# Feed-forward, MLP and output products: one 512-column product per high weight tile in place of two of 256

## The chip, the cores and the metric

The kernel runs on one core of a Trainium2 chip (trn2). The metric is the device time of one execution in microseconds. TensorE multiplies, a stationary operand (weight load) against a moving one whose columns stream through, and adds up in PSUM banks of 512 float32 columns; VectorE and ScalarE read those banks; GpSimd does small work; SyncE issues the weight transfers.

## The reference

Two transformer blocks, one after the other, on one sequence of 256 tokens and 1024 features, all in float32. The first has an attention with compressed, selected and windowed keys beside a gated linear recurrence, then a squared-ReLU MLP; the second has a feed-forward, two attentions (a two-dimensional neighbourhood and a window with a sink), and a second feed-forward. Cut to the products of the change:

```python
def first_block(x, ...):                      # D_MODEL 1024, SEQ 256, D_FF 4096
    ...
    x = x + merged @ w_out[l]
    hn = rms_norm(x, norm2_w[l])
    x = x + jnp.square(jax.nn.relu(hn @ mlp_w1[l])) @ mlp_w2[l]
    return rms_norm(x, final_norm_w)

def swiglu(x, w_gate, w_up, w_down):          # D_FF_2 2816
    return (jax.nn.silu(x @ w_gate) * (x @ w_up)) @ w_down

def second_block(h, ...):
    h = h + 0.5 * swiglu(rms_norm_2(h, ffn1_norm[l]), ffn1_w_gate[l], ffn1_w_up[l], ffn1_w_down[l])
    ...
    h = h + merged @ w_out[l]
    h = h + 0.5 * swiglu(rms_norm_2(h, ffn2_norm[l]), ffn2_w_gate[l], ffn2_w_up[l], ffn2_w_down[l])
    return rms_norm_2(h, final_norm)
```

## The kernel before

Activations lie feature-major: a tile of 128 features by T = 256 tokens. Each float32 operand is cut into a high part, rounded to the format that TensorE multiplies at full rate (float32r), and a low part, the rest. A product W x is then the sum of three: high W by high x, high W by low x, low W by high x. `mm3` (line 271 in the profile) issues these three, each with its own weight load and 256 columns, into one half of a bank: a bank holds a pair of output tiles, 2 x 256 columns. The names in the profile: `f` are the gate and up products of the two feed-forwards (`u2` and `u4` are their inputs, `h` high and `l` low), `fd` the first one's down product, `w` both products of the MLP (inputs `u1` and `hid`), `wo` the two output projections (inputs `m1`, `m2`), `ld` the last down product, which is the other way round: activations stationary, weights moving, 512 columns at first.

Weights stream from memory in pieces of 1024 columns (eight blocks of 128 x 128). For each piece ScalarE makes the high part `whi` (line 221) and VectorE the low part `wlo` (line 222); five of each are kept, and a piece is cut two ahead in program order. A scheduler sets the order on each engine; engines run their queue in order.

When a pair's sum is complete it is read: in the MLP one VectorE operation takes the ReLU and the norm factor `rb_A` (line 1061), ScalarE squares, and both cut the result into the parts of `hid`. In a feed-forward the gate side is multiplied by the norm factor (line 1161), goes through SiLU on ScalarE and is multiplied again (line 1163); the up side is multiplied by it (line 1168) and cut (`f1hi`, `f1lo`). `fm` does products whose sum is added to the residual `res` (line 1041 for `wo`). After `wo`, `w`'s second product and `fd` a norm follows: sums of squares `acc`, a product `ssq_acc` that adds them up over partitions, a small chain of VectorE and GpSimd, and a broadcast `bc_A` on TensorE. The products that need the norm start on features 0 to 5 of 8 before the last two are there.

PSUM has four pools: `g` three banks, `s` two, `t` two, `o` one. Feature-major products take `g`; the up side of a feed-forward takes `s`, which else holds attention scores; `o` holds attention outputs. Line 820, in the first attention, multiplies probabilities of 2 x 384 columns of which it takes the first 256 of each, so that its 512 moving columns are two runs.

Of the kernel before, what the change touches and what calls it, by code (L numbers as in the profile page):

```python
# [9 lines left out]
F32R = mybir.dt.float32r  # L10
# [4 lines left out]
P = 128  # L15
T = 256
# [55 lines left out]
# ------------------------------------------------------------------ constants  # L72
# [81 lines left out]
# Order of the first block's products and of the work between them; "at" takes items of the attention's list.  # L154
# [7 lines left out]
# -------------------------------------------------------------------- program  # L162
class Prog:
    def __init__(self, nc, tc, ctx_pools, d, dbg=None):
# [4 lines left out]
        self.groups = []  # L169

# [61 lines left out]
    def behind(self, ins, before):  # L232
        """keeps ins behind another instruction of its engine"""
# [5 lines left out]
    def table(self, group, **kw):  # L239
        """An activation whose function table is shared by a group: groups are issued in the order of the program."""  # L240
# [22 lines left out]
    def mm3(self, out, wh, wl, xh, xl, start, stop, wside=True):  # L263
        """out += W^T x with operands in two exact parts (W stationary, or x when wside is False)."""
        mm = self.nc.tensor.matmul
        if wside:
            seq = ((wh, xh), (wh, xl), (wl, xh))
        else:
            seq = ((xh, wh), (xh, wl), (xl, wh))
        for r, (a, b) in enumerate(seq):  # L270
# [1280 lines left out]
```

## Time and profile before

| | us |
|---|---|
| three runs, median (lowest to highest) | 994.73 (992.94 to 994.96) |
| profiled execution, span | 992.9 |
| TensorE busy | 982.1 (99%) |
| VectorE busy | 676.7 (68%) |
| ScalarE busy | 549.6 (55%) |
| GpSimd busy | 39.3 (4%) |

The span runs from the first to the last instruction of the profiled execution; the profile has no other time for that execution, and its span lies 1.9 us under the median of the runs. Products on TensorE are pipelined: one is listed at 0.28 us, but the next starts 0.12 us after it, so it is the distance of starts that tells what one costs. The granted clock is at its upper level nearly throughout (mean 0.994).

### The profile page before, as it was taken

The numbers are of one execution on the slowest core, as the hardware profiler recorded it, in microseconds if no ns is written. First come the engines' busy times: TensorE is split into PE (matmuls) and PEld (weight loads), VectorE is DVE, ScalarE is ACT, GpSimd is POOL, SyncE is SP. The second block draws the span as 40 slices with busy tenths as digits, with TensorE's granted clock in tenths as the row PEclk, the third lists the DMA queues.
The fourth block names the chain that finished last, engine by engine and source line by source line (L and its number), as shares of the span: only waits on it lengthen the run. The fifth ranks groups of instructions, "written<-read, shape, count | busy, mean of one in ns | idle before, by whom it ended". The sixth has DMA issues, their size and how long they took to land.

```text
span 992.9 us, 18648 instructions
## 1 busy us (share of the span) xinstructions
PE 982.1 (99%) x7830; PEld 959.4 (97%) x7830; DVE 676.7 (68%) x1051; ACT 549.6 (55%) x833; POOL 39.3 (4%) x71
## 2 busy tenths in 40 slices
PE   8999999999999999999999999999999999999997
PEld 7999999999999999999999999999899999999897
DVE  7898779668666545577666556778767766656453
ACT  6784798446655444455444444667664554444441
POOL 6100000000000000020000200000000000000000
PEclk9999999999999999999999999999999999999999
DMA  8585423635545544555455655442235555555541
GB/s 322 182 296 185 149 105 121 233 127 197 185 170 177 199 177 175 194 176 210 173 196 184 205 191 186 166 170 98 93 108 173 192 204 175 176 200 174 175 154 43
DMA packets 26564, 174.20 MB, mean 175 GB/s; under 512 B 3312, under 2 KB 3568, under 8 KB 7280
## 3 DMA queue, kind: packets, MB, share of 16 engines
q1 hardware_dynamic: 24912, 169.80, 48.2%
q0 software_dynamic: 1136, 2.63, 1.3%
q8 instruction: 61, 1.00, 0.4%
q10 hardware_dynamic: 432, 0.58, 0.2%
q14 instruction: 23, 0.19, 0.1%
HBM read 171.43 MB, written 1.05 MB: 174 GB/s over the span
## 4 chain that ended last, share of the span: by engine, by line
PE 96%; ACT 2%; DVE 1%; DMA 1%; issue 0%; POOL 0%; POOLq 0%; ACTq 0%
PE f L271 26%; PE w L271 19%; PE fd L271 6%; PE ld L271 6%; PE ga L271 5%; PE gb L271 5%; PE wo L271 5%; PE gr L271 3%; PE m1b L271 2%; PE xr L271 2%; PE va L271 1%; PE qb L271 1%; PE qa L271 1%; PE ka L271 1%; PE m1a L271 1%; PE m2b L271 1%
## 5 line engine op out<-in xcount | busy, mean ns | idle before, releaser
L221 ACT ACTIVATE whi<-raw 128x1024 fp32r<-128x1024 f32 (+3 forms) x322 | 336.3, 1048 | 365.2 <-PE f L271 96.2
L222 DVE TENSOR_TENSOR wlo<-raw,whi 128x1024 fp32r<-128x1024 f32 (+3 forms) x322 | 388.6, 1210 | 187.2 <-ACT whi L221 184.3
L271 PE MATMUL f<-u4l,whi 128*128 128x256 f32 x352 | 99.8, 283 | 0.0
L271 PE MATMUL f<-u2h,whi 128*128 128x256 f32 x352 | 99.8, 283 | 0.0
L271 PE MATMUL f<-u4h,wlo 128*128 128x256 f32 x352 | 99.6, 283 | 0.0
L271 PE MATMUL f<-u4h,whi 128*128 128x256 f32 x352 | 99.6, 283 | 0.0
L271 PE MATMUL f<-u2l,whi 128*128 128x256 f32 x352 | 99.6, 283 | 0.0
L271 PE MATMUL f<-u2h,wlo 128*128 128x256 f32 x352 | 99.6, 283 | 0.0
L271 PE MATMUL w<-u1h,wlo 128*128 128x256 f32 x256 | 72.6, 284 | 0.0
L271 PE MATMUL w<-hid_hi,whi 128*128 128x256 f32 x256 | 72.4, 283 | 0.0
L271 PE MATMUL w<-hid_lo,whi 128*128 128x256 f32 x256 | 72.4, 283 | 0.0
L271 PE MATMUL w<-hid_hi,wlo 128*128 128x256 f32 x256 | 72.4, 283 | 0.0
L271 PE MATMUL w<-u1h,whi 128*128 128x256 f32 x256 | 72.4, 283 | 0.0
L271 PE MATMUL w<-u1l,whi 128*128 128x256 f32 x256 | 72.4, 283 | 0.0
L271 PEld LDWEIGHTS f<-u4h,wlo 128*128 128x128 f32 x352 | 67.6, 192 | 0.0
L271 PEld LDWEIGHTS f<-u2l,whi 128*128 128x128 f32 x352 | 67.6, 192 | 0.0
L271 PEld LDWEIGHTS f<-u4h,whi 128*128 128x128 f32 x352 | 67.6, 192 | 0.0
L271 PEld LDWEIGHTS f<-u2h,whi 128*128 128x128 f32 x352 | 67.6, 192 | 0.0
L271 PEld LDWEIGHTS f<-u4l,whi 128*128 128x128 f32 x352 | 67.6, 192 | 0.0
L271 PEld LDWEIGHTS f<-u2h,wlo 128*128 128x128 f32 x352 | 67.6, 192 | 0.0
L271 PE MATMUL fd<-f1hi,whi 128*128 128x256 f32 x176 | 49.8, 283 | 0.0
L271 PE MATMUL fd<-f1lo,whi 128*128 128x256 f32 x176 | 49.8, 283 | 0.0
(598 smaller groups left out, 2746.1 us busy)
## 6 DMA issues: line engine op xcount, KB each, us to landing
raw<-in_ws_dram SPq DMA_DIRECT2D x150, 1024.0 KB, 4.9
raw<-in_ws_dram SPq DMA_DIRECT2D x3, 960.0 KB, 4.8
raw<-in_ws_dram SPq DMA_DIRECT2D x2, 992.0 KB, 5.2
nar<-in_rpb_dram POOLq DMA_DIRECT2D x16, 96.0 KB, 5.4
raw<-in_ws_dram SPq DMA_DIRECT2D x4, 256.0 KB, 7.2
raw<-in_ws_dram SPq DMA_DIRECT2D x2, 512.0 KB, 7.3
raw<-in_ws_dram SPq DMA_DIRECT2D x1, 932.0 KB, 4.8
res<-in_x_dram SPq DMA_DIRECT2D x2, 384.0 KB, 7.0
```

Source lines behind the costliest of these rows:

```text
L221: self.hi_ins.append(nc.scalar.activation(out=hi[:, :w], in_=src, func=AF.Copy))
L222: nc.vector.tensor_tensor(out=lo[:, :w], in0=src, in1=hi[:, :w].bitcast(F32), op=ALU.subtract)
L271: mm(out, a, b, start=start and r == 0, stop=stop and r == 2, skip_group_check=True)
```

## The change

A block's two products with the high weight become one: the two parts of an activation lie behind one another in one buffer (`Parts`: per four feature tiles one buffer, high parts in the first half, low parts in the second), and both stream past one weight load as 512 columns, two runs of 256 (`mm_wide`). High by high lands in the first half of a bank, high by low in the second; the product with the low weight adds 256 columns to the first half. So an output tile takes a whole bank and a pair two. `banks` takes them in rotation from `g`, `g`, `g`, `s`, `s`, `o`. Whoever reads a pair now sums the halves: `fold` lets ScalarE copy the second half to SBUF and VectorE add the first; `add_res` adds both halves to the residual one after the other. This is done for `wo`, `w`, `f` and `fd`; all other feature-major products keep three products per block (`mmx`). Comments are taken out, and the buffers of parts of other operands (`u0`, `xcp`, `rnn`, `ya`, `yb`, ...) are cut in the new way too.

```diff
+WIDE = ("g", "g", "g", "s", "s", "o")
+class Parts:
+    def buf(self, k):
+        while len(self.bufs) <= k // 4:
+            self.bufs.append(self.big(f"{self.name}_{len(self.bufs)}", F32R, (P, 2, 4, T)))
+        return self.bufs[k // 4]
+    def both(self, k):
+        return self.buf(k)[:, :, k % 4, :]
...
+    def mm_wide(self, bank, wh, wl, x, start, stop):
+        mm = self.nc.tensor.matmul
+        mm(bank.rearrange("p (a t) -> p a t", a=2), wh, x, start=start, stop=False, skip_group_check=True)
+        mm(bank[:, :T], wl, x[:, 0, :], start=False, stop=stop, skip_group_check=True)
+
+    def banks(self, name):
+        out = []
+        for nn in range(2):
+            tag = WIDE[self.n_wide % len(WIDE)]
+            self.n_wide += 1
+            out.append(self.ps(tag, f"{name}_{nn}"))
+        return out
+
+    def fold(self, out, bs):
+        for nn, b in enumerate(bs):
+            o = out[:, nn * T:(nn + 1) * T]
+            self.nc.scalar.activation(out=o, in_=b[:, T:], func=AF.Copy)
+            self.nc.vector.tensor_tensor(out=o, in0=b[:, :T], in1=o, op=ALU.add)
...
 (fm, fm_norm, ffn)
-                    st[p] = self.ps(pool, f"{tag}_{p}")
-                b = st[p]
+                    st[p] = self.banks(f"{tag}_{p}")
                 for k in range(k0, k1):
-                    xh, xl = x(k)
                     for nn in range(2):
                         wh, wl = self.wt((tag, k, 2 * p + nn))
-                        self.mm3(b[:, nn * T:(nn + 1) * T], wh, wl, xh, xl, k == 0 and nn == 0, k == nk - 1)
+                        self.mm_wide(st[p][nn], wh, wl, x(k), k == 0, k == nk - 1)
...
+    def add_res(p, bs, fac):
+        for nn, b in enumerate(bs):
+            r = S["res"][:, 2 * p + nn, :]
+            for a in range(2):
+                nc.vector.scalar_tensor_tensor(out=r, in0=b[:, a * T:(a + 1) * T], scalar=fac, in1=r, op0=ALU.mult, op1=ALU.add)
...
-    def ev_mlp(p, b):
+    def ev_mlp(p, bs):
...
-        nc.vector.scalar_tensor_tensor(out=v2(r), in0=v2(b), scalar=0.0, in1=two(S["rbA"]), op0=ALU.max, op1=ALU.mult)
+        G.fold(r, bs)
+        nc.vector.scalar_tensor_tensor(out=v2(r), in0=v2(r), scalar=0.0, in1=two(S["rbA"]), op0=ALU.max, op1=ALU.mult)
...
-        def ev(p, side, b):
+        def ev(p, side, bs):
...
-                nc.vector.tensor_tensor(out=v2(s), in0=v2(b), in1=two(S["rbA"]), op=ALU.mult)
+                G.fold(s, bs)
+                nc.vector.tensor_tensor(out=v2(s), in0=v2(s), in1=two(S["rbA"]), op=ALU.mult)
...
-                nc.vector.tensor_tensor(out=h, in0=b, in1=s, op=ALU.mult)
-                q = p % 4
-                G.split2(pair(S["hh"][p // 4], q), pair(S["hl"][p // 4], q), v2(h))
+                G.fold(h, bs)
+                nc.vector.tensor_tensor(out=h, in0=h, in1=s, op=ALU.mult)
+                G.split2(*S["hid"].pair(p), v2(h))
```

What this does to the order of instructions, at three places. First TensorE in the first feed-forward, the end of the gate side of pair 4 (`f10_4`: feed-forward 1, side 0) and the first product of its up side (`f11_4`); the numbers in `whi156` and `wlo156` are those of weight pieces. Before:

```order
L271 MATMUL f10_4_5574<-u2h_4281,wlo156_5543 128x256
L271 MATMUL f10_4_5574<-u2h_4281,whi156_5542 128x256
L271 MATMUL f10_4_5574<-u2l_4282,whi156_5542 128x256
L271 MATMUL f10_4_5574<-u2h_4281,wlo156_5543 128x256
L271 MATMUL f11_4_5639<-u2h_4281,whi157_5575 128x256
L271 MATMUL f11_4_5639<-u2l_4282,whi157_5575 128x256
L271 MATMUL f11_4_5639<-u2h_4281,wlo157_5576 128x256
```

and now:

```order
L306 MATMUL f10_4_0_5022<-u2_1_4368,whi156_4994 128x512
L307 MATMUL f10_4_0_5022<-u2_1_4368,wlo156_4995 128x256
L306 MATMUL f10_4_1_5023<-u2_1_4368,whi156_4994 128x512
L307 MATMUL f10_4_1_5023<-u2_1_4368,wlo156_4995 128x256
L306 MATMUL f11_4_0_5074<-u2_0_3999,whi157_5024 128x512
L307 MATMUL f11_4_0_5074<-u2_0_3999,wlo157_5025 128x256
L306 MATMUL f11_4_1_5075<-u2_0_3999,whi157_5024 128x512
```

Three products per block are two, and the two tiles of a pair go to two banks (`f10_4_0`, `f10_4_1`).

Second VectorE at the same pair; `f1s4` and `f1h4` are the SBUF buffers of its gate and up side. Before:

```order
L222 TENSOR_TENSOR wlo160_5671<-raw83_5540,whi160_5670 128x1024
L1161 TENSOR_TENSOR f1s4_5635<-f10_4_5574,rb_A2_5159 128x512
L222 TENSOR_TENSOR wlo161_5704<-raw83_5540,whi161_5703 128x1024
L1163 TENSOR_TENSOR f1s4_5635<-f1s4_5635,rb_A2_5159 128x512
L222 TENSOR_TENSOR wlo162_5734<-raw84_5603,whi162_5733 128x1024
L1168 TENSOR_TENSOR f1h4_5698<-f11_4_5639,f1s4_5635 128x512
L222 TENSOR_TENSOR wlo163_5767<-raw84_5603,whi163_5766 128x1024
L278 TENSOR_TENSOR f1lo4_5634<-f1h4_5698,f1hi4_5633 128x512
```

and now (L323 is the fold's add, L1198, L1200 and L1206 are the old L1161, L1163 and L1168):

```order
L249 TENSOR_TENSOR wlo160_5099<-raw83_4992,whi160_5098 128x1024
L330 TENSOR_TENSOR f1h_1_4915<-f1h3_5014,f1h_1_4915 128x512
L323 TENSOR_TENSOR f1s4_5066<-f10_4_0_5022,f1s4_5066 128x256
L249 TENSOR_TENSOR wlo161_5130<-raw83_4992,whi161_5129 128x1024
L323 TENSOR_TENSOR f1s4_5066<-f10_4_1_5023,f1s4_5066 128x256
L1198 TENSOR_TENSOR f1s4_5066<-f1s4_5066,rb_A2_4669 128x512
L249 TENSOR_TENSOR wlo162_5152<-raw84_5044,whi162_5151 128x1024
L1200 TENSOR_TENSOR f1s4_5066<-f1s4_5066,rb_A2_4669 128x512
L323 TENSOR_TENSOR f1h4_5118<-f11_4_0_5074,f1h4_5118 128x256
L249 TENSOR_TENSOR wlo163_5182<-raw84_5044,whi163_5181 128x1024
L323 TENSOR_TENSOR f1h4_5118<-f11_4_1_5075,f1h4_5118 128x256
L1206 TENSOR_TENSOR f1h4_5118<-f1h4_5118,f1s4_5066 128x512
```

Two adds stand ahead of each first read, and that read takes SBUF in place of the bank; the splits of the weights keep their distance.

Third VectorE at the start of the MLP, where its norm ends (`ssq_acc1` to `rb_A`); `mr0` to `mr2` are the buffers of the first pairs, `w1_0_0` is a bank of pair 0. Before:

```order
L443 TENSOR_TENSOR acc1_2844<-acc1_2844 128x256
L222 TENSOR_TENSOR wlo81_3147<-raw43_2962,whi81_3146 128x1024
L483 COPY sscA_3110<-ssq_acc1_3106 128x2
L416 TENSOR_SCALAR v_A_3112<-sscA_3110 128x2
L222 TENSOR_TENSOR wlo82_3177<-raw44_3029,whi82_3176 128x1024
L222 TENSOR_TENSOR wlo83_3211<-raw44_3029,whi83_3210 128x1024
L1061 SCALAR_TENSOR_TENSOR mr0_3123<-w1_0_3000,rb_A_3119 128x512
L1061 SCALAR_TENSOR_TENSOR mr1_3140<-w1_1_3047,rb_A_3119 128x512
L222 TENSOR_TENSOR wlo84_3241<-raw45_3088,whi84_3240 128x1024
L278 TENSOR_TENSOR hid_lo0_3122<-mr0_3123,hid_hi0_3121 128x512
```

and now:

```order
L249 TENSOR_TENSOR wlo83_3131<-raw44_2974,whi83_3130 128x1024
L323 TENSOR_TENSOR mr0_3047<-w1_0_0_2952,mr0_3047 128x256
L323 TENSOR_TENSOR mr0_3047<-w1_0_1_2953,mr0_3047 128x256
L323 TENSOR_TENSOR mr1_3065<-w1_1_0_2988,mr1_3065 128x256
L532 COPY sscA_3036<-ssq_acc1_3032 128x2
L466 TENSOR_SCALAR v_A_3038<-sscA_3036 128x2
L249 TENSOR_TENSOR wlo84_3153<-raw45_3018,whi84_3152 128x1024
L323 TENSOR_TENSOR mr1_3065<-w1_1_1_2989,mr1_3065 128x256
L323 TENSOR_TENSOR mr2_3118<-w1_2_0_3074,mr2_3118 128x256
L249 TENSOR_TENSOR wlo85_3184<-raw45_3018,whi85_3183 128x1024
L323 TENSOR_TENSOR mr2_3118<-w1_2_1_3075,mr2_3118 128x256
L1106 SCALAR_TENSOR_TENSOR mr0_3047<-mr0_3047,rb_A_3045 128x512
```

The folds of the first pairs do not need the norm and now stand ahead of `rb_A`, partly ahead of the copy of the sums of squares; before, the bank's first reader waited for `rb_A`.

## Rows read from the trace of the kernel before

**Rows 1.** The page, sections 1 and 4: busy time by engine, the last chain.

```profile
PE 982.1 (99%) x7830; PEld 959.4 (97%) x7830; DVE 676.7 (68%) x1051; ACT 549.6 (55%) x833; POOL 39.3 (4%) x71
...
PE 96%; ACT 2%; DVE 1%; DMA 1%; issue 0%; POOL 0%; POOLq 0%; ACTq 0%
```

**Rows 2.** Stretches: length, PE, PEld, DVE, ACT, POOL busy us (count), PEclk, DMA.

```profile
249.50:338.00 88.50, 88.50 (x740) 88.50 (x739) 59.03 (x63) 50.73 (x64) 0.00 (x0) 1.00 0.51 179
...
439.95:550.10 110.15, 110.15 (x920) 110.15 (x920) 76.25 (x88) 53.24 (x63) 1.30 (x2) 1.00 0.55 190
```

**Rows 3.** Timeline, start us, length us: first and last of 34 starts, down product.

```profile
560.01 0.28 PE L271 MATMUL fd<-f1hi,whi 128*128 128x256 f32 x1
...
563.97 0.28 PE L271 MATMUL fd<-f1hi,whi 128*128 128x256 f32 x1
```

**Rows 4.** Timeline: first and last of ten starts, last product, 512 columns.

```profile
935.09 0.39 PE L271 MATMUL ld<-whi,f2hi 128*128 128x512 f32 x1
...
937.13 0.39 PE L271 MATMUL ld<-whi,f2hi 128*128 128x512 f32 x1
```

**Rows 5.** Groups by operands, TensorE, xcount | busy us, mean ns of one.

```profile
L271 PE MATMUL f<-u4l,whi 128*128 128x256 f32 x352 | 99.8, 283 | 0.0
...
L271 PE MATMUL w<-u1h,whi 128*128 128x256 f32 x256 | 72.4, 283 | 0.0
...
L271 PE MATMUL fd<-f1hi,whi 128*128 128x256 f32 x176 | 49.8, 283 | 0.0
...
L271 PE MATMUL wo<-m2h,whi 128*128 128x256 f32 x64 | 18.1, 283 | 0.0
```

**Rows 6.** Timeline, TensorE: 512 columns in two runs (L820), in one after a wait.

```profile
194.76 0.63 PE L820 MATMUL o<-pt021h,v 128*128 128x512 f32 x2
195.23 0.27 PE L753 MATMUL ptn<-ident,attn 128*128 128x128 f32 x1
...
200.61 0.62 PE L820 MATMUL o<-pt121h,v 128*128 128x512 f32 x2
201.07 0.28 PE L271 MATMUL m1b<-rnn_hi,whi 128*128 128x256 f32 x1
...
929.61 0.40 PE L271 MATMUL ld<-whi,f2hi 128*128 128x512 f32 x1
929.85 0.40 PE L271 MATMUL ld<-wlo,f2hi 128*128 128x512 f32 x1
```

**Rows 7.** Groups, VectorE, 440 to 550 us, first feed-forward.

```profile
L222 DVE TENSOR_TENSOR wlo<-raw,whi 128x1024 fp32r<-128x1024 f32 x38 | 46.5, 1225 | 22.7 <-ACT whi L221 22.7
L1161 DVE TENSOR_TENSOR f1s<-f,rb_A 128x512 f32<-128x512 f32 x11 | 7.6, 690 | 5.7 <-PE f L271 5.1 <-ACT rb_A L454 0.6
L1163 DVE TENSOR_TENSOR f1s<-f1s,rb_A 128x512 f32<-128x512 f32 x11 | 7.5, 684 | 0.0
```

**Rows 8.** Groups, VectorE, 214 to 250 us, output product and norm.

```profile
L281 DVE SCALAR_TENSOR_TENSOR u1l<-res,vec,u1h 128x256 fp32r<-128x256 f32 x8 | 3.4, 478 | 0.0
L1041 DVE SCALAR_TENSOR_TENSOR res<-wo,res 128x512 f32<-128x512 f32 x4 | 2.8, 690 | 0.3 <-PE wo L271 0.3
...
L443 DVE TENSOR_TENSOR acc<-acc 128x256 f32<-128x256 f32 x1 | 0.4, 419 | 0.0
```

**Rows 9.** Groups, ScalarE, 440 to 550 us.

```profile
L221 ACT ACTIVATE whi<-raw 128x1024 fp32r<-128x1024 f32 x38 | 40.3, 1061 | 55.0 <-PE f L271 36.9 <-issue 18.0
...
L454 ACT ACTIVATE rb_A<-bc_A 128x256 f32<-128x256 f32 x1 | 0.4, 383 | 1.4 <-PE bc_A L452 1.4
```

**Rows 10.** Timeline, TensorE: sum of squares and broadcast, first feed-forward.

```profile
431.99 0.95 PE L445 MATMUL ssq_acc<-ones,acc 128*128 128x2 f32 x8
...
439.35 0.38 PE L452 MATMUL bc_A<-ident,rs_fh 128*128 128x128 f32 x2
```

**Rows 11.** View by stretches: attention and recurrence, first MLP product.

```profile
100.00:150.00 50.00, 50.00 (x385) 47.39 (x385) 39.08 (x96) 44.40 (x94) 0.00 (x0) 0.99 0.35 129
250.00:300.00 50.00, 50.00 (x419) 50.00 (x419) 34.59 (x38) 29.55 (x39) 0.00 (x0) 1.00 0.51 175
```

More of the change, by code (lines that the diff above doesn't have):

```diff
@@ L159, with __init__, tile, pair @@
 ma2 mb2 ma3 mb3"""
+class Parts:
+    def __init__(self, big, name):
+        self.big, self.name, self.bufs = big, name, []
+    def buf(self, k):
[4 more added lines that the diff above has]
+        return self.buf(k)[:, :, k % 4, :]
+    def tile(self, k):
+        return [self.buf(k)[:, a, k % 4, :] for a in range(2)]
+    def pair(self, p):
+        q = 2 * p % 4
+        return [self.buf(2 * p)[:, a, q:q + 2, :] for a in range(2)]
 class Prog:
@@ L281, in split2, with fm @@
             nc.vector.scalar_tensor_tensor(out=lo, in0=src, scalar=scale, in1=hi.bitcast(F32), op0=ALU.mult, op1=ALU.subtract)
-    def fm(self, tag, name, nk, npair, x, evac, rows=None, cols=None, lead=2, hold=2, after=None, pool="g"):
+    def fm(self, tag, name, nk, npair, x, evac, rows=None, cols=None, lead=2, hold=2, after=None):
         rows = rows or (lambda k: [(k * P, P)])
@@ L488, in build @@
     G.step(setup)
-    xu = lambda k: (S["u0h"][:, k, :], S["u0l"][:, k, :])
+    xu = lambda k: S["u0"].both(k)
     def norm0():
@@ L574, in vg @@
             wh, wl = G.wt(("vg", k))
+            xh, xl = S["u0"].tile(k)
             for i in range(2):
                 sl = slice(i * P, (i + 1) * P)
[L577 removed]
+                G.mm3(banks[i][:, :280], wh, wl, xh[:, sl], xl[:, sl], k == 0, k == 7)
         for i in range(2):
@@ L828, in nsa_out @@
     def nsa_out(p):
-        S["aoh"], S["aol"] = S["q"][:, 0], S["q"][:, 1]
-        G.split2(pair(S["aoh"], p), pair(S["aol"], p), v2(S["o1"]))
+        G.split2(*(pair(S["q"][:, a], p) for a in range(2)), v2(S["o1"]))
     def rnn_prep():
@@ L1017, in merge @@
         return branch
-    m1 = merge("m1", "w_up_attn", "w_up_rnn", 4, 8, lambda k: (S["aoh"][:, k, :], S["aol"][:, k, :]),
-               lambda k: (S["rnh"][:, k, :], S["rnl"][:, k, :]), paired, plain)
+    m1 = merge("m1", "w_up_attn", "w_up_rnn", 4, 8, lambda k: S["q"][:, :, k, :],
+               lambda k: S["rnn"].both(k), paired, plain)
     PARTS_1 = {
@@ L1035, in build, with ev @@
             PARTS_1[w[:-1]](int(w[-1]))
+    def add_res(p, bs, fac):
[3 more added lines that the diff above has]
+                nc.vector.scalar_tensor_tensor(out=r, in0=b[:, a * T:(a + 1) * T], scalar=fac, in1=r, op0=ALU.mult, op1=ALU.add)
     def out_proj(tag, name, x, fac, nxt):
-        def ev(p, b):
-            r = pair(S["res"], p)
-            nc.vector.scalar_tensor_tensor(out=r, in0=v2(b), scalar=fac, in1=r, op0=ALU.mult, op1=ALU.add)
+        def ev(p, bs):
+            add_res(p, bs, fac)
             nxt(p)
@@ L1181, in build, with ev_f1 @@
     nin = norm_in("u3", "mix", "acc1")
-    def ev_f1(p, b):
-        r = pair(S["res"], p)
-        nc.vector.scalar_tensor_tensor(out=r, in0=v2(b), scalar=0.5, in1=r, op0=ALU.mult, op1=ALU.add)
+    def ev_f1(p, bs):
+        add_res(p, bs, 0.5)
         nin(p)
-    G.fm("fd", "ffn1_w_down_2", 22, 4, lambda k: (hid("hh", k), hid("hl", k)), ev_f1, lead=0)
+    G.fm("fd", "ffn1_w_down_2", 22, 4, xof("hid"), ev_f1, lead=0)
     W2 = "w_in_2"
@@ L1285, in va @@
         for k in range(8):
-            xh, xl = x3(k)
+            xh, xl = S["u3"].tile(k)
             for c in range(2):
@@ L1367, in b2_tail @@
         if j == 0:
-            S[f"y{kind}h"], S[f"y{kind}l"] = both("y" + kind, (4, T))
+            S["y" + kind] = Parts(G.big, "y" + kind)
         if j % 2 == 1:
-            G.split2(pair(S[f"y{kind}h"], j // 2), pair(S[f"y{kind}l"], j // 2), v2(S["o2"]))
+            G.split2(*S["y" + kind].pair(j // 2), v2(S["o2"]))
     def ev_g2(key):
```

107 lines of the change are left out of this document (43 added, 64 removed).

## The prediction

> **What bounds the kernel now.** I read the busy shares first, then the chain that ended last, then stretches, then single products. The busy shares have TensorE at 99% of the span and VectorE at 68%, and the chain is 96% TensorE [rows 1]. A busy TensorE need not be at its peak, so the next view is that of stretches: in a long stretch of the squared-ReLU MLP's first product (249.5 to 338 us) 740 products start in 88.5 us, in the first feed-forward (from 439.95 us) 920 in 110.15 us, one each 0.120 us without a gap, the granted clock at its upper level of 2.4 GHz throughout; VectorE works 59 of 88.5 us and 76 of 110.15 us there [rows 2]. So in these stretches nothing but the number and length of TensorE's products counts, as long as the other engines keep up.
>
> The single products say what one is made of. 33 products of 256 columns lie between 560.01 and 563.97 us: 0.120 us each [rows 3]. Nine of 512 columns lie between 935.09 and 937.13 us: 0.2267 us each [rows 4]. The 256 columns between the two cost 106.7 ns, one column per cycle of 2.4 GHz, and so each product has a fixed part of 120.0 - 106.7 = 13.3 ns beside its columns. It is there at both widths.
>
> **The change, part by part.**
> *The products.* Each weight block [128 x 128] in the MLP, the feed-forwards' gate, up and first down product and the two output projections now takes one product of 512 columns and one of 256 instead of three of 256. Columns stay at 768 per block. The blocks: 11 pairs x 2 tiles x 8 x 2 sides = 352 for each feed-forward, 256 for each of the MLP's two products, 176 for the down product and 64 for each output projection, each of them one product in every group of the view by operands, which shows three groups per tensor (high part with high weight, low with high, high with low) and of which one per tensor stands in [rows 5]; f, w and wo each name two tensors of that name. In all 2 x 352 + 2 x 256 + 176 + 2 x 64 = 1520. A block goes from 3 x 120.0 = 360.0 ns to 226.7 + 120.0 = 346.7 ns, 13.3 ns less, and 1520 x 13.3 = **20.3 us**, all on the path that sets the end.
>
> The new product reads its 512 columns in two runs of 256. Line 820 does the same (two runs, 384 apart) and bounds the price: two such products go from 200.61 to 201.07 us, two from 194.76 to 195.23, 0.23 to 0.235 us each [rows 6]. But a product of 512 columns in one run shows the same shortly after a wait, 0.24 us from 929.61 to 929.85, and 0.227 later [rows 6, 4]. I take 226.7 ns, since the wide products stand in long gapless stretches, as those of [rows 4] do, and not singly in a stage with waits as line 820's; 0.235 us is the upper end, 0.2267 the lower, as no row has less.
>
> *The folds.* A pair of output tiles now fills two banks (high sum in one half, low part's sum in the other) and 60 pairs (16 in the MLP, 22 in each feed-forward) get, for each bank, a ScalarE copy of 256 columns out of PSUM and a VectorE add of 256. Rows: such a copy takes 0.383 us [rows 9], an add of that size out of SBUF 0.419 us [rows 8]. The trace has no plain add of 256 that reads PSUM; at 512 columns the one that reads PSUM takes 0.690 and the one that doesn't 0.684 us [rows 7], so 0.42 it is, with 0.478, the slowest of 256 [rows 8], as upper end. Per pair: ScalarE +0.77, VectorE +0.84 us. VectorE now has two weight splits of 1.225, and two of the 0.69 kind, 3.83 us per pair of 5.76; it will have 4.67 of 16 x 0.3467 = 5.55 us. ScalarE has 50.73 / 88.5 x 5.76 = 3.30 and will have 4.07 us. Both fit, VectorE at 84%. The cover is therefore real but thin: 0.88 us per pair; were it gone, each further 0.1 us per pair would cost 60 x 0.1 = 6 us.
>
> VectorE's in-order queue does block on a fold until TensorE has ended the pair. In the excerpts the gate of pair 4 ends with piece 156 on TensorE, and its fold stands behind the split of piece 160 on VectorE; four pieces are 4 x 8 x 0.347 = 11.1 us of products, so the block itself starves nothing.
>
> *The residual updates.* One update of 512 columns, 0.690 us, becomes four of 256, at 0.478 us each [rows 8]: +1.22 us per pair, 16 pairs, 19.6 us of VectorE in all. Beside 5.55 us of products and more per pair it is hidden; only the last pair of a stage leads on to the norm. There 24 blocks, 24 x 0.347 = 8.3 us, need nothing of it, and in the second excerpt of VectorE's order the copy of the sum of squares now stands behind the fold of the MLP's second pair, whose first tile is complete after 31 blocks, 10.7 us, where it stood ahead of the first read. Price 0, at most 1.2 us at each of four stage ends, 5 us.
>
> *Banks.* The rotation of six banks holds three pairs. A feed-forward had three banks for gates and two for ups, five pairs. A pair's banks are wanted again two pairs later, 11.1 us, and the fold does not wait for the norm, whose chain takes 7.4 us from the sum of squares to the broadcast [rows 10]. Before, the read of the bank waited for that norm. I take 0; a gain of up to 1 us is possible from the short stalls at the broadcasts.
>
> The Trainium skill speaks against this part: "Mind PSUM pressure: TensorE tiling speeds up compute but not PSUM evacuation" (Trainium Kernel Development and Optimization, Best Practices). The trace agrees that evacuation is what grows, from 2 x 0.69 = 1.38 to 2.22 us per pair of VectorE, while products shrink by 4%; with the third of VectorE that is free in [rows 2] it decides nothing unless the slow rival below is true.
>
> *The attention between.* No product there changes, but buffers of two tensors' parts are cut otherwise, and the scheduler orders gr, gb and the attention's tails anew. That stage is not gapless: 385 products in 100 to 150 us against 419 in 250 to 300 [rows 11], 34 x 0.12 = 4 us that can grow or shrink. I take 0, with 3 us either way.
>
> **Sum.** 992.9 us of the profiled span - 20.3 = 972.6. The median of the three runs, 994.73, stands 1.9 us above that span, so **974.4 us**.
>
> **Rivals.**
> 1. *The two runs cost.* If every wide product took 235 ns, the block would be at 355 ns, the saving 1520 x 5 = 7.6 us, the time 987.1; at a half of that price 980.8. For it: line 820's 0.23 to 0.235 us. Against: the one-run product after a wait has 0.24.
> 2. *The fixed part does not go with the instruction.* If it belonged to the columns, 120.0 / 256 = 0.469 ns each, a wide product would take 240 ns and nothing would be saved: 994.7, the change not doing what it says. Against: 0.2267 us in [rows 4]. In a milder form a fifth of the 13.3 ns, 2.7 ns, goes with the instruction and the rest stays with the block: 1520 x 2.7 = 4.1 us, 990.6. The Trainium skill has a rule of that size: back to back, N / 2.4 + 2.5 ns (TensorE: Matmul & The Clock Gate, Back-to-back issue gap); by it an estimated 1520 x 2.5 = 3.8 us would go. The trace disagrees with it by 10.8 ns at both widths.
> 3. *VectorE becomes the bound, slower.* Place: the 60 pairs. A fold's add needs ScalarE's copy, which can stand behind a weight copy of 1.061 us [rows 9]; if VectorE idled 1.061 + 0.383 = 1.44 us per pair, it would need 4.67 + 1.44 = 6.11 us, 0.56 over TensorE's 5.55, and 60 x 0.56 = 34 us would be lost against 20.3 saved: 1008 us. It decides from 20.3 / 60 = 0.34 us over 5.55 per pair, a wait of 1.2 us. For it: the copy and the weight copy do share a queue. Against: the splits are four pieces ahead, so VectorE can wait for a while and catch up.
>
> **How the numbers follow.** Forecast 0.81 (own range 970.4 to 980: the attention's 3 us and up to 1 at the broadcasts down, 5 at the stage ends up), two runs 0.08, fixed part 0.06 (no saving 0.03, the mild form 0.03), VectorE 0.05. The range 970.4 to 984 takes in the lower half of the first rival. What can be told from no change here is about 0.2%, 2 us. Faster: 0.81 + 0.08 + 0.03 = 0.92; same 0.03; slower 0.05.
>
> **What would show it.** Right: 1520 fewer product records (7830 to about 6310), wide ones starting 0.227 us before the next and blocks 0.347 us apart, the first feed-forward's 110 us down by 4, VectorE busy about 60 x 0.84 + 19.6 = 70 us more and ScalarE 46 us more, TensorE still 96% or so of the chain. Wrong: pitches of 0.23 to 0.24 in gapless stretches (first rival) or of 0.24 (second); waits of TensorE for a bank or for a low weight part every pair, with VectorE near 100% in the MLP (third). A stall at the start of the MLP or a feed-forward alone would only cost the few us of the range.

## The result and the profile after

The changed kernel takes 980.4 us (median of four runs, 979.5 to 980.6), the kernel before 993.96 us beside it (four runs, 992.94 to 994.96). The ratio is 0.9865, with a 95% interval of [0.9851, 0.9879]: faster, by 13.6 us, where the prediction gave 974.4 us, 20.3 us less. The profiled execution has a span of 977.7 us, 15.1 less than the 992.9 of before. Runs of the kernel before fall near 993.0 or near 994.8 us, mostly at a mean granted clock of 0.998 and of 0.994, so medians of a few runs can lie up to 1.8 us apart without any edit, and the argument below goes by stages.

Sections 1 and 4 of the page after, which answer to [rows 1]:

```profile
PE 962.3 (98%) x6310; PEld 874.2 (89%) x6310; DVE 729.8 (75%) x1219; ACT 580.4 (59%) x953; POOL 40.1 (4%) x71
...
PE 97%; DVE 1%; DMA 1%; ACT 0%; issue 0%; SPq 0%; POOL 0%; POOLq 0%
```

1520 products fewer, and TensorE is still what the chain consists of. VectorE's share rose by seven points. What is new is that TensorE is at 98 and not 99%: it idles somewhere.

In the first feed-forward's down product, where [rows 3] had a start every 0.120 us, the timeline (start us, length us) now reads:

```profile
559.62 0.39 PE L306 MATMUL fd<-f1h,whi 128*128 128x512 f32 x1
559.86 0.28 PE L307 MATMUL fd<-f1h,wlo 128*128 128x256 f32 x1
559.97 0.40 PE L306 MATMUL fd<-f1h,whi 128*128 128x512 f32 x1
...
562.05 0.40 PE L306 MATMUL fd<-f1h,whi 128*128 128x512 f32 x1
```

Seven blocks lie between the first and the last of these starts: 2.43 us / 7 = 0.347 us each. For the whole program a table by stage is of more use. It takes a stage from the start of its first product to that of the next stage's, us, from the two timelines (the last one from the transposes ahead of it to the start of its last product); beside it stands what 13.3 ns for each of its wide blocks would make.

| stage | before | after | change | by 13.3 ns a block |
|---|---|---|---|---|
| block 1 up to wo | 212.44 | 211.22 | -1.22 | 0 |
| wo and wo2 | 46.08 | 44.54 | -1.54 | -1.71 |
| w1 | 92.81 | 89.53 | -3.28 | -3.41 |
| w2 | 92.16 | 88.75 | -3.41 | -3.41 |
| f1 gate, up | 128.03 | 123.53 | -4.50 | -4.69 |
| fd | 63.36 | 61.01 | -2.35 | -2.35 |
| mixer of block 2 | 158.66 | 162.51 | +3.85 | 0 |
| f2 gate, up | 127.38 | 124.73 | -2.65 | -4.69 |
| last product | 63.31 | 63.29 | -0.02 | 0 |

Two lines hold most of what is missing: the mixer, where no product was changed, lost 3.85 us, and f2 gained 2.0 us less than its blocks should give, 1.85 less than f1, which has the same code. The first line is not the change's: it is a dip of the granted clock that one of the two executions has (see the last section).

**The mixer.** The view of waits (engine, line, waited for: us in total, times, longest) has one row for TensorE between 595 and 625 us; before, the same place (610 to 640 us) has none:

```profile
PE ka L300 <- DVE qa L1258: 3.3, 1, 3.3
```

The two pairs of qa and the two of ka share a pool of three banks, so the second pair of ka needs a bank that still holds a pair of qa, and VectorE evacuates that one only once it has the norm. So the norm is late. VectorE's timeline after shows why (the last down product ends at 597.8 us; in brackets the idle time ahead of an instruction and its releaser):

```profile
597.35 1.75 DVE L1242 TENSOR_TENSOR nab<-cst,nar 128x1536 f32<-128x1536 f32 x1
599.02 0.75 DVE L1086 SCALAR_TENSOR_TENSOR res<-fd,res 128x256 f32<-128x256 f32 x2
599.68 1.22 DVE L249 TENSOR_TENSOR wlo<-raw,whi 128x1024 fp32r<-128x1024 f32 x1
600.82 0.75 DVE L1086 SCALAR_TENSOR_TENSOR res<-fd,res 128x256 f32<-128x256 f32 x2
...
608.75 1.75 DVE L1242 TENSOR_TENSOR nab<-cst,nar 128x1536 f32<-128x1536 f32 x1
610.42 0.15 DVE L532 COPY sscA<-ssq_acc 128x2 f32<-128x2 f32 x1
610.89 1.16 DVE L249 TENSOR_TENSOR wlo<-raw,whi 128x960 fp32r<-128x960 f32 x1 [0.32 <-ACT whi L248]
611.96 0.16 DVE L466 TENSOR_SCALAR v_A<-sscA 128x2 f32<-128x2 f32 x1
```

Two subtractions of 1.75 us that build the attention's bias table (nab) now stand right ahead of the last residual updates and of the norm's two small steps. Before, they ran well inside the down product, 31 and 18 us ahead of qa's start; the view of the tile has (shortest, median and longest ns, first and last start us):

```profile
L1206 DVE TENSOR_TENSOR nab<-cst,nar x2: 1749/1750/1751, 582.4 to 595.5; 128x1536 f32<-128x1536 f32 x2
```

TensorE's timeline has the sum of squares 11.0 us behind qa's start (8.2 before) and the broadcast 17.6 us behind it (12.2 before). The kernel before (qa starts at 613.29 us) first, then the changed one (597.76 us):

```profile
621.45 0.50 PE L445 MATMUL ssq_acc<-ones,acc 128*128 128x2 f32 x4
...
625.49 0.38 PE L452 MATMUL bc_A<-ident,rs_A 128*128 128x128 f32 x2
```

```profile
608.78 0.51 PE L495 MATMUL ssq_acc<-ones,acc 128*128 128x2 f32 x4
...
615.34 0.38 PE L502 MATMUL bc_A<-ident,rs_A 128*128 128x128 f32 x2
```

The price is more than the wait. The view by stretches (length, busy us of PE, PEld, DVE, ACT, POOL with counts, granted clock, DMA share, GB/s) has the idle stretch and the one behind it:

```profile
615.40:619.00 3.60, 0.44 (x4) 0.24 (x2) 2.42 (x5) 1.28 (x2) 0.00 (x0) 0.96 0.44 120
619.00:622.50 3.50, 3.35 (x17) 3.38 (x18) 3.37 (x7) 3.34 (x6) 0.00 (x0) 0.55 0.64 265
622.50:626.00 3.50, 3.50 (x32) 3.50 (x31) 2.64 (x4) 2.70 (x4) 0.00 (x0) 1.00 0.03 5
```

Behind the idle stretch the granted clock is 0.55 (mostly its lower level, 1.2 GHz): 17 products start where the next 3.5 us have 32. With its last product ka is 4.85 us late against before. Behind it 1.0 us comes back: the products of va and eight of the scores Sa, the same as before, take that much less, Sa's eight now in one go and not among va's. That leaves 3.85 us.

**f2.** Around its norm's broadcast the timeline after reads:

```profile
798.95 0.40 PE L306 MATMUL f<-u,whi 128*128 128x512 f32 x1
799.18 0.28 PE L307 MATMUL f<-u,wlo 128*128 128x256 f32 x1
799.30 0.38 PE L502 MATMUL bc_A<-ident,rs_A 128*128 128x128 f32 x2
799.44 0.47 PE L306 MATMUL f<-u,whi 128*128 128x512 f32 x1
...
800.58 0.40 PE L306 MATMUL f<-u,whi 128*128 128x512 f32 x1
...
801.64 0.40 PE L306 MATMUL f<-u,whi 128*128 128x512 f32 x1
```

From 800.58 to 801.64 are three blocks, 1.06 us, 353 ns each; the blocks between the sum of squares and this broadcast took 347. The unrounded starts show a pattern of three blocks (232 + 118, 241 + 120, 236 + 113 ns), here called the slow rhythm, that lasts from here to the end of f2; w2 and fd run in pairs of 230 + 117 ns, the fast one. 353.3 - 346.7 = 6.6 ns over the 305 blocks from here on are the missing 2.0 us. TensorE waits for no engine there, and the granted clock is 1.00.

### The profile page after: what moved, and what is told of

The parts are those of the page before. It is cut to its first block, busy times and chain, and to the rows that moved or that the text cites. A ratio compares the mean times of both kernels' runs of the same rounds, so it can differ in the third digit from the quotient of the medians.

```text
span 977.7 us, 15978 instructions
## 1 busy us (share of the span) xinstructions
PE 962.3 (98%) x6310; PEld 874.2 (89%) x6310; DVE 729.8 (75%) x1219; ACT 580.4 (59%) x953; POOL 40.1 (4%) x71
## 4 chain that ended last, share of the span: by engine, by line
PE 97%; DVE 1%; DMA 1%; ACT 0%; issue 0%; SPq 0%; POOL 0%; POOLq 0%
PE f L306 17%; PE w L306 12%; PE f L307 8%; PE w L307 6%; PE ld L294 6%; PE ga L300 5%; PE gb L300 5%; PE fd L306 4%; PE wo L306 3%; PE gr L300 2%; PE m1b L300 2%; PE xr L300 2%; PE fd L307 2%; PE wo L307 2%; PE va L294 1%; PE ka L300 1%
## 5 line engine op out<-in xcount | busy, mean ns | idle before, releaser
L306 PE MATMUL f<-u,whi 128*128 128x512 f32 x704 | 246.7, 396 | 0.0
L307 PE MATMUL f<-u,wlo 128*128 128x256 f32 x704 | 196.9, 280 | 0.0
L306 PEld LDWEIGHTS f<-u,whi 128*128 128x128 f32 x704 | 132.2, 188 | 31.2
L307 PEld LDWEIGHTS f<-u,wlo 128*128 128x128 f32 x704 | 132.9, 189 | 0.1
L306 PE MATMUL w<-u,whi 128*128 128x512 f32 x256 | 88.8, 392 | 0.0
L306 PE MATMUL w<-hid,whi 128*128 128x512 f32 x256 | 88.8, 391 | 0.0
L307 PE MATMUL w<-hid,wlo 128*128 128x256 f32 x256 | 71.9, 281 | 0.0
L307 PE MATMUL w<-u,wlo 128*128 128x256 f32 x256 | 71.5, 281 | 0.0
L306 PE MATMUL fd<-f1h,whi 128*128 128x512 f32 x176 | 61.1, 394 | 0.0
L294 PE MATMUL ld<-whi,f2h 128*128 128x256 f32 (+1 forms) x264 | 59.1, 319 | 0.0
L306 PEld LDWEIGHTS w<-hid,whi 128*128 128x128 f32 x256 | 47.9, 187 | 10.4
L306 PEld LDWEIGHTS w<-u,whi 128*128 128x128 f32 x256 | 47.8, 187 | 10.2
L306 PE MATMUL wo<-m,whi 128*128 128x512 f32 x128 | 44.4, 394 | 0.0
```

The lines of the kernel that those rows point to most:

```text
L306: mm(bank.rearrange("p (a t) -> p a t", a=2), wh, x, start=start, stop=False, skip_group_check=True)
L307: mm(bank[:, :T], wl, x[:, 0, :], start=False, stop=stop, skip_group_check=True)
```

## The experiments

Every time below stands beside runs of the kernel before on the same chip, and the ratio is to those (the changed kernel has 0.9865). The expectations of e7 and e8 start from 993.2 us for the kernel before, the median beside e1 to e4; beside e5 to e8 it took 994.65.

**e1_table_early.** The step that loads the bias table and its constants stands ahead of the down product:

```
+    G.step(lambda: constants("cst2", CONST_2))
+    G.step(bias_load)
     G.fm("fd", "ffn1_w_down_2", 22, 4, xof("hid"), ev_f1, lead=0)
 ...
-    G.step(lambda: constants("cst2", CONST_2))
-    G.step(bias_load)
```

> The mixer's constants and its bias table (two VectorE subtractions of 1.75 us, which in the changed kernel run at 597.4 and 608.7 us, around the last residual updates and the norm) are issued ahead of the feed-forward's output product. Theory A (these subtractions make the mixer's norm late, ka's second pair then waits 3.3 us for a bank and the clock halves behind it): the wait of ka behind qa goes, the mixer's products take about 158.7 us instead of 162.5, and the time falls from 980.4 to 975 to 977 us. Rival B (the residual updates in four parts are late by themselves): the wait stays, at most 1.5 us shorter, 979 to 980 us. Rival C (the missing gain lies in the products with two runs): no change, 980.4 us.

976.11 us (975.5 to 977.83), ratio 0.9828 [0.9815, 0.9842]. Theory A holds: the mixer takes 158.66 us, to the hundredth what it took before, and TensorE waits for no qa. On VectorE's timeline the four-part update runs at once and the sum's copy waits only for its product:

```profile
599.11 1.44 DVE L1086 SCALAR_TENSOR_TENSOR res<-fd,res 128x256 f32<-128x256 f32 x4 [0.17 <-PE fd L307]
600.47 1.22 DVE L249 TENSOR_TENSOR wlo<-raw,whi 128x1024 fp32r<-128x1024 f32 x1
...
607.95 0.16 DVE L532 COPY sscA<-ssq_acc 128x2 f32<-128x2 f32 x1 [0.48 <-PE ssq_acc L495]
608.15 0.17 DVE L466 TENSOR_SCALAR v_A<-sscA 128x2 f32<-128x2 f32 x1
```

Broadcast 12.2 us behind qa's start, as before. So rival B falls as well: the update in four parts, still there, costs nothing here. Rival C falls with the time. The profiled span fell by 2.3 us only, since block 1's attention took 1.5 us more than in the changed kernel's profile (see the last section).

**e2_three.** Folds, banks and layout as changed, the wide product split:

```
-        mm(bank.rearrange("p (a t) -> p a t", a=2), wh, x, start=start, stop=False, ...)
+        mm(bank[:, :T], wh, x[:, 0, :], start=start, stop=False, ...)
+        mm(bank[:, T:], wh, x[:, 1, :], start=False, stop=False, ...)
```

> As the changed kernel, banks, folds and layout included, but the 512-column product is two of 256 columns on the same high weight tile, into the two bank halves. Theory A (a product saves its fixed 13.3 ns and nothing else): 1520 x 13.3 = 20.3 us come back, less the 2.3 us that f2's products lose in the changed kernel: about 998.4 us, 4 us over the kernel before. Rival B (the new folds and updates cost time only because the products are shorter): with 360 ns a block VectorE has more cover, 994 us, as the kernel before. Rival C (the wide product saves less than 13.3 ns): 985 to 992 us.

997.08 us (995.95 to 999.92), ratio 1.0042 [1.0026, 1.0058]. Theory A. w1, w2, f1, fd, f2 take 92.82, 92.16, 128.03, 63.36 and 127.38 us, within 0.01 us of before, folds and all; the mixer takes 161.2 us and has the 3.3 us wait for qa. So without the wide product the rest of the change is a loss; what of it the profiled execution shows is in the mixer, 2.55 us, and that execution is the fastest of the four. The folds cost nothing, at 360 ns a block as at 346.7.

**e3_contig.** High and low part of a feature tile lie beside each other: one run of 512 columns.

```
-            self.bufs.append(self.big(..., F32R, (P, 2, 4, T)))
+            self.bufs.append(self.big(..., F32R, (P, 4, 2, T)))
```

> The high and the low part of one feature tile lie beside each other, so that the moving operand of the wide product is one run of 512 columns instead of two of 256. Theory A (two runs cost nothing): blocks stay at 346.7 ns, f2's at 353, 980.4 us within 1. Rival B (f2's slower three-block pattern comes from the two runs): f2 falls by 2.3 us, 978 us. Rival C (each second run costs some ns): all 1520 blocks become shorter, by 3 ns or more, 976 us or less.

980.68 us (979.88 to 981.33), ratio 0.9872 [0.9859, 0.9886]. Theory A: no stage differs by over 0.5 us from the changed kernel, f2 takes 124.73 us again. Two runs cost nothing, and f2's slow blocks don't come from them.

**e4_fold_more.** One more VectorE operation in each fold:

```
             self.nc.vector.tensor_tensor(out=o, in0=b[:, :T], in1=o, op=ALU.add)
+            self.nc.vector.tensor_tensor(out=o, in0=o, in1=o, op=ALU.max)
```

> Each fold has one more VectorE operation of 128x256 from and to SBUF (the larger of the fold's result and itself, which changes no value), 120 in all. Theory A (VectorE needs 4.67 of 5.55 us a pair in f1): with the acc row's 0.42 us it needs 5.5 of 5.55 us, still hidden in the dense part; 980.4 to 984 us. Rival B (VectorE's work is already late for the banks): every added 0.42 us shows, up to 120 x 0.42 = 50 us, 1000 us or more. If the operation on SBUF alone is faster than 0.42 us, no change.

984.44 us (984.02 to 984.73), ratio 0.991 [0.9897, 0.9924], 4 us more than changed. That looks like VectorE at its edge, but it isn't where the time went. f1 and f2 have folds in all their 44 pairs and are 0.2 and 0.0 us longer; w1 is 1.3 and w2, which has no fold at all, 1.7 us longer, and block 1's attention, with the clock dip of the last section, 1.8. The stretches of w2 and f1, the same columns as above:

```profile
336.00:416.00 80.00, 80.00 (x455) 69.36 (x454) 43.27 (x51) 36.40 (x44) 0.00 (x0) 1.00 0.53 185
440.00:520.00 80.00, 80.00 (x464) 70.01 (x463) 75.92 (x126) 47.95 (x76) 1.30 (x2) 1.00 0.56 196
```

In f1 VectorE is busy 75.92 of 80 us, 95%, and TensorE still starts 464 products; in w2 VectorE is half idle and TensorE starts 455 (the changed kernel 464 in 330 to 410 us): f2's slow rhythm, here in another stage. The folds' cover held to the end of what was tried.

**e5_bank_s.** Norm and table late as in the changed kernel, ka's second pair in another pool's bank:

```
-                S[tag, p] = G.ps("g", f"{tag}{p}")
+                S[tag, p] = G.ps("s" if (tag, p) == ("ka", 1) else "g", f"{tag}{p}")
```

> As the changed kernel, but the second pair of ka accumulates in a bank of pool s and not in the third bank of pool g, which qa's evacuation holds; norm and tables stay where they are. Theory A (the late norm costs time only through ka's wait for that bank): the wait of 3.3 us and the half clock behind it go, and the mixer's products fall from 162.5 us to between 158.7 and 159.5; 976 to 977 us. Rival B (whatever comes after the norm is late by as much, so the wait moves to the scores behind ka): the mixer stays at 161 us or more, 979 to 980.5 us.

976.55 us (975.51 to 977.57), ratio 0.982 [0.9805, 0.9834]. Theory A: the mixer takes 158.65 us though the broadcast is 17.6 us behind qa's start as in the changed kernel. TensorE's timeline goes straight on:

```profile
615.18 0.38 PE L502 MATMUL bc_A<-ident,rs_A 128*128 128x128 f32 x2
615.32 0.37 PE L300 MATMUL ka<-u,wlo 128*128 128x256 f32 x1
615.52 0.41 PE L300 MATMUL ka<-u,whi 128*128 128x256 f32 x2
615.76 0.29 PE L300 MATMUL ka<-u,wlo 128*128 128x256 f32 x1
```

So the loss is a chain with two links, and taking away either undoes it: the table ahead of the norm (e1), and a bank that is not free before the norm (e5).

**e6_one_swap.** e1, and in a single block of f2 the low tile's product goes first:

```
+        if swap:   # pair 1, gate, k = 1, first tile of f2
+            mm(bank[:, :T], wl, x[:, 0, :], start=False, stop=False, ...)
+            mm(bank.rearrange("p (a t) -> p a t", a=2), wh, x, start=False, stop=stop, ...)
+            return
```

> e1_table_early, with one block of f2 (behind its norm, of 704 blocks in the stage's and f1's code) that issues the low tile's 256-column product ahead of the 512-column one. Theory A (f2's blocks of 353 ns are a rhythm that begins where the norm's transposes stood between two blocks, and lasts until the next interruption; in f1 they stood inside a block and the rhythm ended there): one block in another order ends it, f2 falls from 124.7 to about 122.7 us, and the time from 976.1 to 974 us. Rival B (f2's place in memory or its weights make its products slower): f2 stays at 124.7 us, 976.1 us. Rival C (the swap ends the rhythm but another as slow begins): as B in time, with another sequence of pitches.

974.68 us (973.67 to 975.47), ratio 0.98 [0.9786, 0.9815]. f2 takes 122.72 us, 4.66 us less than before: 13.3 ns for nearly each of its 352 blocks. The slow rhythm isn't there, and nothing else changed: but for these two products the traces of e1 and e6 have the same instructions in the same order on TensorE, VectorE and ScalarE. The stretches of f2, the changed kernel first, then e6:

```profile
802.00:902.00 100.00, 100.00 (x569) 86.77 (x568) 79.28 (x110) 59.11 (x93) 0.00 (x0) 1.00 0.55 189
```

```profile
802.00:902.00 100.00, 100.00 (x578) 88.18 (x578) 81.04 (x113) 59.46 (x93) 0.00 (x0) 1.00 0.55 189
```

Rival B falls: place and weights are the same. So does C. But the expectation put the block behind the norm, and in the timeline it (L305, L306) stands between the norm's sum of squares (791.21) and its broadcast (797.22):

```profile
791.21 0.50 PE L497 MATMUL ssq_acc<-ones,acc 128*128 128x2 f32 x4
...
792.70 0.28 PE L305 MATMUL f<-u,wlo 128*128 128x256 f32 x1
792.82 0.40 PE L306 MATMUL f<-u,whi 128*128 128x512 f32 x1
...
797.22 0.38 PE L504 MATMUL bc_A<-ident,rs_A 128*128 128x128 f32 x2
```

So it did not end a slow rhythm; none began. It did change the pattern that ran: the unrounded starts ahead of it are 233, 117, 231 and 113 ns apart (347 ns a block), behind it 230 and 117, and that goes on behind the broadcast to the end of f2. In e1 the first pattern runs up to the broadcast, and the slow rhythm follows.

**e7_outputs_only** and **e12_outputs_banks.** The four output products wide, w1, f1 and f2 with three products and no fold:

```
-                        G.mm_wide(st[p, side][nn], wh, wl, x(k), k == 0, k == 7)
+                        G.mmx(st[p, side][:, nn * T:(nn + 1) * T], wh, wl, x(k), k == 0 and nn == 0, k == 7)
 ...
+                    st[p, side] = G.ps("g", ...)                   # e7
+                    st[p, side] = G.ps(("g", "s")[side], ...)      # e12, as before the change
```

> Only the four output products (wo, w2, fd, wo2: 560 blocks) are wide with their banks and four-part residual updates; w1, f1 and f2 have three products a block, one bank a pair and no fold, as before. Theory A (13.3 ns a block, and the mixer's table as in the changed kernel stands ahead of the last residual update and of the norm): 560 x 13.3 = 7.5 us less, 3.9 us lost in the mixer: 993.2 - 7.5 + 3.9 = 989.6 us. Rival B (the folds of f1 made the mixer's norm late, not the four-part updates or the table): no loss in the mixer, 985.7 us.

997.64 us (995.79 to 999.45), ratio 1.0032 [1.0018, 1.0046]: slower than before, and neither theory's number. The mixer lost 5.05 us (the wait of ka, and the granted clock at 0.5 behind it for twice as long), so rival B falls: the folds of f1 aren't needed for the table to be late. The slow rhythm took 1.7 us in w2 and 1.2 in fd. And w1 and f1 lost 1.3 and 1.5 us that nobody had forecast. In f1 the suspect was an oversight: e7 had put gates and ups into one pool of three banks, where the kernel before has two more. e12 mends that.

> e7_outputs_only with the ups of f1 and f2 in the two banks of pool s, as in the kernel before; in e7 they shared the three banks of pool g with the gates. Theory A (f1's loss of 1.5 us in e7 came from those fewer banks alone, w1's of 1.3 us from the updates): f1 at 128.0 us again, w1 still at 94.1, the mixer still with ka's wait; 997.6 - 1.5 = 996.1 us. Rival B (the four-part updates of w2 make f1's norm late, whatever the banks): f1 stays at 129 us or more, 997.6 us.

995.36 us (994.59 to 998.1, ten runs), ratio 1.0017 [1.0007, 1.0027]. Theory A: f1 takes 128.03 us as before, w1 still 94.12, the mixer 162.68. The view of waits of this kernel:

```profile
PE ka L300 <- DVE qa L1255: 3.3, 1, 3.3
...
PE w L300 <- DVE u L333: 0.8, 1, 0.8
```

w1 waits 0.8 us for the parts that follow a four-part residual update. So a wait at a stage end of the size that the prediction allowed for does exist, in this kernel; the changed kernel has none there. The 7.5 us that 560 blocks save are all lost again: 2.9 us to the rhythm, 1.3 in w1, 4.0 in the mixer.

**e8_folds_only.** The reverse: w1, f1, f2 wide, the output products with three products and one update of 512 columns.

```
-                        self.mm_wide(st[p][nn], wh, wl, x(k), k == 0, k == nk - 1)
+                        self.mmx(st[p][:, nn * T:(nn + 1) * T], wh, wl, x(k), k == 0 and nn == 0, k == nk - 1)
```

> Only w1, f1 and f2 (960 blocks) are wide, with banks and folds; the output products have three products a block and one residual update a pair, as before. Theory A: 960 x 13.3 = 12.8 us less, 2.1 us lost in f2, and with the table one step earlier on VectorE and the residual update in one piece no wait of ka: 993.2 - 12.8 + 2.1 = 982.5 us, mixer at 158.7. Rival B (the folds cost more than they hide): above 984 us, w1 or f1 longer than in the changed kernel. Rival C (the fold side alone makes the mixer late): 986 us, the wait of ka is there.

986.98 us (985.85 to 987.04), ratio 0.9922 [0.9907, 0.9937]; expected 982.5, or 984.0 from the 994.65 beside it. The mixer is at 158.67 us as theory A had it (the table's subtractions run ahead of the last update and behind the norm's steps: 604.79 and 619.17 us, with qa's start at 608.2). What theory A missed is that f1 has the slow rhythm as well, 125.54 us instead of 123.53. The forecast took it for f2's own.

**e9_zigzag.** e1, with every second wide block turned (wide, low, low, wide):

```
+        self.n_mm += 1
+        first, second = (wide, low) if self.n_mm % 2 else (low, wide)
```

> e1_table_early with every second wide block (all stages) issuing the low tile's product first: wide, low, low, wide. Theory A (the slow rhythm of 353 ns belongs to the strict alternation of 512 and 256 columns, and no rhythm arises where the order turns at each block): all blocks at 346.7 ns, also the ones around the norms, f2 at 122.7 us and w1, f1 up to 0.4 us shorter each: 974 us. Rival B (the rhythm is set by whatever interrupts the products, in any order): f2 stays at 124.7 us or another stage takes the slow rhythm instead (256 blocks of w2 are worth 1.7 us): 976 to 978 us. Rival C (a change of order costs at each turn, 5 ns or more): 1520 x 5 / 2 = 3.8 us more, 980 us.

977.74 us (976.21 to 978.11), ratio 0.9831 [0.9815, 0.9848]. No stage has the slow rhythm, f2 takes 123.31 us, but w2 takes 89.17 instead of 88.75: 256 blocks at 348.3 ns, 1.6 ns over e1's. A piece of A and a small piece of C: one middling rhythm everywhere, and no gain over e1.

**e10_two_swaps** and **e11_late_swap.** Meant: e6's block and a second one half way through f2, and that second one alone:

```
-(tag, p, side, k, nn) == ("f2", 1, 0, 1, 0)
+(tag, p, side, k, nn) in (("f2", 1, 0, 1, 0), ("f2", 11, 0, 1, 0))    # e10
+(tag, p, side, k, nn) == ("f2", 11, 0, 1, 0)                          # e11
```

The edit does not do what it was meant to. A feed-forward has 11 pairs on each side, numbered 0 to 10, and the expectations take it for 22: pair 11 does not exist, and no second block is turned. The view by line of e10 has one product on the turned block's line, e6's; that of e11 has all 704 blocks of f1 and f2 on the line of the usual order (shortest, median and longest ns, first and last start us, shape with the number of samples):

```profile
L305 PE MATMUL f<-u,wlo x1: 278/278/278, 792.4 to 792.4; 128*128 128x256 f32 x1
```

```profile
L308 PE MATMUL f<-u,whi x704: 390/395/481, 415.0 to 904.9; 128*128 128x512 f32 x176
```

So e10 is e6 once more and e11 is e1, instruction by instruction on TensorE, VectorE and ScalarE.

> e6_one_swap with a second block of f2 turned, half way through the stage (pair 11 of 22). Theory A (the rhythm of 346.7 ns is stable, and a turned block leaves it alone): f2 at 122.7 us, 974.7 us. Rival B (a turned block toggles between two rhythms): f2's second half at 353 ns, 176 x 6.6 = 1.2 us more, 975.9 us.

974.51 us (973.97 to 975.16), ratio 0.9802 [0.9788, 0.9817], f2 122.72 us, as in e6 to the hundredth. Neither theory was tested.

> e1_table_early with one turned block (low tile's product first) in the middle of f2 alone (pair 11 of 22), where f2 runs at 353 ns a block; in e6_one_swap the turned block stood between the norm's sum of squares and its broadcast, before the slow rhythm could begin. Theory A (a turned block ends a slow rhythm that is under way): the second half of f2 runs at 346.7 ns, f2 at 124.7 - 176 x 6.6 ns = 123.5 us, the time from 976.1 to about 975 us. Rival B (only what stands at an interruption of the products decides, and a turned block changes nothing later): f2 stays at 124.7 us, 976.1 us.

976.81 us (975.93 to 977.47), ratio 0.9824 [0.9808, 0.9841], f2 124.73 us, as in e1 to the hundredth. Neither theory was tested here either: whether a block turned in the middle of a stage changes a rhythm, slow or fast, stays open. What the two runs show is that the rhythms come again: the same program takes the same one in a second profile.

## Why the prediction was right, and where it was off

**Products: right in mechanism and in size.** 346.7 ns a block is what w2 and fd show, to the hundredth of a microsecond of their stages; e2, which undoes this alone, gives it all back. Only the sum came out, not its two terms: the starts stand 230.0 and 116.7 ns apart, where the forecast had 226.7 and 120.0. With both losses taken away (e6) the stages with wide products are together 19.7 us shorter than before, of 20.3 forecast, and the time is 974.68 us, 20.0 less than before beside it.

**The total: in the range, in part by luck.** 980.4 us lies above the forecast's own range (to 980) and within the stated one (to 984), which was stretched to take in half of the first rival. That rival's half price gives 980.8 us, nearly the time measured, and e3 shows that its mechanism had no part in it: what was lost went to the two terms that follow.

**The term that was mis-sized within it: 13.3 ns for all 1520 blocks.** In f2 the blocks after the norm saved 6.7. The pitch was read from stretches of equal products [rows 3, 4]; the trace of before has no stretch in which 512 and 256 columns alternate. A hint was there: the row at 929.61 us in [rows 6], taken for one after a wait, stands behind eight transposes of htok, without a wait of TensorE, and there some ten products of 512 columns in one run stand 224 to 236 ns apart before 227 sets in. The forecast priced a wide product between two pitches, but not a pair of products that can keep either of two.

**Residual updates: the failing step, "Price 0, at most 1.2 us at each of four stage ends".** The updates themselves took 0.42 us each, not 0.478, and cost nothing in the changed kernel (e1), though in e12 w1 lost 1.3 us with them, about the step's bound. The step looked at the updates' own length and, of the order, at the norm of w1; in the mixer the scheduler had put two instructions of 1.75 us ahead of the norm, and that order was there to be read. 3.85 us at one place, over three times the step's bound: the wait for a bank and then a lower clock, which the step had not thought of as a price. Why the scheduler moved the table isn't settled. It is late in e2, e7 and e12, which share with the changed kernel the four-part updates, and early enough in e8, which does without them.

**Folds: right.** ScalarE's copies took 0.38 us and VectorE's adds 0.42, as taken from [rows 8, 9]. The lengths of all operations rose by 67 us on VectorE and 45 on ScalarE (70 and 46 forecast), the busy time by 53 and 31, as operations that overlap are counted once. The cover was real, and less thin than thought: at 95% VectorE nothing was lost (e4). The slow rival had no part in it.

**Banks: right.** No product of w1, f1 or f2 waits for a bank in the changed kernel; e7 against e12 shows what too few cost, 1.5 us in f1. That matters, for the norms of w1 and f2 are late too: their broadcasts stand 19.6 and 16.8 us behind the stage's start (12.2 and 11.7 before), and no product waits. The folds there empty the banks without the norm; the evacuation of qa in the mixer can't.

**Attention: -1.2 us,** inside the 3 us allowed, but no gain of the change: the profile of before has a dip of the granted clock there, that of the changed kernel none (last section). e1, with such a dip, takes 212.72 us for this stage, before 212.44.

**Rivals.** Two runs cost nothing (e3). The fixed part goes with the instruction, as [rows 3, 4] said: w2, without stall or rhythm, fell by 3.41 us, 256 x 13.3 ns. The Trainium skill's rule of N / 2.4 + 2.5 ns (TensorE: Matmul & The Clock Gate, Back-to-back issue gap), which that section gives as the gap of an isolated product and not of a stream with its weight loads, would have made an estimated 256 x 2.5 ns = 0.64 us there; the trace disagrees. The sentence that f1's 110 us would be down by 4 held (whole stage -4.50).

What is missing in the end: 20.3 forecast, less 3.85 (mixer) and 2.0 (f2), less 0.5 spread over f1, w1 and the output products, plus 1.2 in the attention, the clock's, is the 15.1 us of the two spans. Of the 0.5, f1's part is 0.2, and 0.15 of that are its 22 blocks between the sum of squares and the broadcast, which run in the slow rhythm too; behind the broadcast f1 has the fast one.

## What to carry to other kernels

Where a change lengthens what stands on an engine ahead of a norm, read that engine's order at every place where the norm is needed, for the long instructions that have nothing to do with the change: a scheduler moves them too. A pair of products with unequal widths can run at more than one steady pitch, so price it from a stretch of such pairs, or leave a few ns a block in the range; and a total that comes out wrong is taken apart by stage before any cause is named (e4's 4 us were none of the engine that was loaded).

## What the runs showed of the hardware

- Alternating 512- and 256-column products ran at 346.7 or at 353.3 ns a block, each steady for 60 us and more, at a granted clock of 1.00, and with the same instructions: w2 in e1 and in e4, f1 in e1 and e8, f2 in e6 and e1. Equal products (three of 256 a block) showed one pitch only, 120.0 ns, in every long dense stretch of before and of e2. In f2 of e1, f1 of e8 and w1 of e4 the slow rhythm set in right behind the norm's broadcast, and in e4 it ran on through w2. e6 against e1 (and e10 against e11, the same two programs once more) shows that the order of one block's two products, ahead of the broadcast, decides which rhythm follows; what selects it stays open. Where the broadcast stands (between two blocks or inside one) does not decide it alone, as in f1 of the changed kernel it stands inside a block and the fast pitch follows, and in f1 of e8 it does too and the slow one follows.
- The 3.3 us of waiting cost 3.85 us net, with products at about half their rate in the 3.5 us behind it. In block 1's attention the granted clock dips in some profiled executions and not in others; the stretch of 94 to 102 us, the kernel before first, then the changed kernel, then e1, has 0.79, 1.00 and 0.79, and 52, 64 and 51 products:

```profile
94.00:102.00 8.00, 8.00 (x52) 7.40 (x51) 5.40 (x16) 2.25 (x3) 0.00 (x0) 0.79 0.37 133
```

```profile
94.00:102.00 8.00, 8.00 (x64) 7.49 (x63) 6.64 (x18) 3.73 (x8) 0.00 (x0) 1.00 0.38 133
```

```profile
94.00:102.00 8.00, 8.00 (x51) 7.48 (x50) 5.67 (x17) 2.23 (x3) 0.00 (x0) 0.79 0.38 134
```

In e1's profile the stage is 1.5 us longer than in the changed kernel's, though no edit touched it, and that hides over a third of the 3.85 us that e1 gained.
